# GLU over 8192 x 8192: the group's store and the reload of its buffer each issued as two transfers over even and odd partitions, and fewer, larger instructions per load

## The chip, the cores and the metric

The kernel runs on one core of a Trainium2 chip. The metric is the device time of one execution in microseconds. Before the change three timed runs gave 950.84 us as their median (947.65 to 954.41).

## The reference

The input `x` has 8192 rows of 8192 fp32 values. Each row is cut in two halves a and b, and the output, 8192 x 4096, is a times the sigmoid of b:

```python
def reference(x):
    a, b = np.split(x, 2, axis=-1)
    return a * (1 / (1 + np.exp(-b)))
```

The kernel reads 268.44 MB and writes 134.22 MB. There is one sigmoid and one multiplication per output value and no reuse of anything.

## The kernel before, in words

**Groups and halves.** The 8192 rows are cut into 16 groups of 512 rows. Of a group, each of the 128 partitions owns four neighbouring rows of x (128 KiB of device memory), split into two halves h = 0 and h = 1 of two rows each. A half is one load: 128 partitions by 64 KiB, 8.39 MB. The group's output, four packed rows of 16 KiB per partition, is again 64 KiB per partition, and normally leaves as one store of 8.39 MB.

**Three slots.** SBUF holds three buffers (slots) of 64 KiB per partition. Half 1 of every group uses slot 1. Half 0 uses slot 0 in even groups and slot 2 in odd groups, and the products of both halves are written packed into the slot of half 0, over data that has already been read. So slot 0 or 2 is loaded, worked on, filled with the whole group's output, stored, and only then loaded again, with half 0 of the group after the next one.

**Work.** `work` (L56) handles a quarter of a half at a time: 2048 columns of one of the two rows. ScalarE takes the sigmoid of b in place (L67), VectorE multiplies a by it and writes the product to its packed place (L71). Where a product would go over a value that an earlier product still has to read, the sigmoid waits for that product.

**Queues and waits.** All loads are issued from SyncE (L54), all stores from ScalarE (L78); each goes into the DMA queue of its issuing engine, and both queues are served by the same 16 DMA engines. The order of everything is the program's order, and most waits that the framework would add are taken out (`place`, L35); those that are left are these:

```python
load(g + 1, 1, [mul_of[g, 1, 3]])            # slot 1 is free after the group's last product
store(g, 2 if first else 0, 8, mul_of[g, 1, 3])
if g + 2 < n_groups:
    load(g + 2, 0, store_of[g])               # slot 0 or 2 is free when the store has landed
```

The first load is issued in two parts, and group 0 and the last group, 15, store in smaller pieces, so that the output starts and ends in small steps. The functions at the end of the program (`_launch_early`, `_close_on_sync`) move the first load ahead of the start barrier and shorten the end; the change doesn't touch them.

Of the kernel before, what the change touches and what calls it, by code (L numbers as in the profile page):

```python
# [6 lines left out]


def _tiles(ctx, tc, x, out):


    nc = tc.nc
    P = nc.NUM_PARTITIONS
    DEP = mybir.DependencyInfo(mybir.DependencyClass.Sync, mybir.DependencyReason.DATA)
    fp32 = mybir.dt.float32
    SIG = mybir.ActivationFunctionType.Sigmoid

    n_rows, n_cols = x.shape
    half = n_cols // 2
    quarter = half // 2  # L20
    R, H = 2, 2
    n_groups = n_rows // (P * R * H)
    x_t = x.rearrange("(g p h r) m -> g h p (r m)", p=P, h=H, r=R)
    out_t = out.rearrange("(g p q) m -> g p (q m)", p=P, q=H * R)

    pool = ctx.enter_context(tc.tile_pool(name="io", bufs=1))
    slots = [pool.tile([P, R * n_cols], fp32, name=f"x_sb{k}") for k in range(3)]
    traced = [[] for _ in slots]
    load_of, mul_of, store_of = {}, {}, {}

    def slot(g, h):
        return 1 if h else 2 * (g % 2)

    def place(touched, ins, *needs):


        kept = {n.ins.name for n in needs}
        seen = set()
        for k in touched:
            for e in traced[k]:  # L40
                if e.ins.name not in kept | seen:
                    seen.add(e.ins.name)
                    tc.declare_no_dep(ins.ins, e.ins, reason="follows from the waits that are kept")
            traced[k].append(ins)
        tc.keep_in_program_order(ins)
        return ins

    def load(g, h, needs=(), parts=1):

        width = R * n_cols // parts  # L50
        k = slot(g, h)
        for j in range(parts):
            c = slice(j * width, (j + 1) * width)
            ins = place([k], nc.sync.dma_start(out=slots[k][:, c], in_=x_t[g, h][:, c]), *needs)  # L54
            for r in range(R) if parts == 1 else [j]:
                load_of[g, h, r] = ins  # L56

    def work(g, h, k):

        r, c = k // 2, k % 2 * quarter  # L60
        of, to = slot(g, h), slot(g, 0)
        a = slots[of][:, r * n_cols + c : r * n_cols + c + quarter]
        b = slots[of][:, r * n_cols + half + c : r * n_cols + half + c + quarter]
        at = (h * R + r) * half + c
        before = {(0, 2): (g, 0, 0), (0, 3): (g, 0, 1), (1, 0): (g, 0, 3)}
        over = [mul_of[m] for m in [before.get((h, k))] if m]
        sig = nc.scalar.activation(out=b, in_=b, func=SIG)  # L67
        place([of], sig, load_of[g, h, r], *over)
        for m in over:
            tc.add_manual_dep(sig.ins, m.ins.name, DEP, reason="read before the product goes over it")  # L70
        mul = nc.vector.tensor_mul(out=slots[to][:, at : at + quarter], in0=a, in1=b)  # L71
        mul_of[g, h, k] = place(sorted({of, to}), mul, sig)

    def store(g, lo, hi, done):

        c = slice(lo * quarter, hi * quarter)
        k = slot(g, 0)
        ins = place([k], nc.scalar.dma_start(out=out_t[g][:, c], in_=slots[k][:, c]), done)  # L78
        store_of.setdefault(g, []).append(ins)

    load(0, 0, parts=2)
    load(0, 1)
    load(1, 0)
    for g in range(n_groups):
        first, final = g == 0, g == n_groups - 1
        for k in range(4):
            work(g, 0, k)
            if first and k == 1:
                store(g, 0, 2, mul_of[g, 0, 1])
        if final:  # L90
            store(g, 0, 2, mul_of[g, 0, 1])
            store(g, 2, 4, mul_of[g, 0, 3])
        for k in range(4):
            work(g, 1, k)
            if final and k > 0:
                store(g, 3 + k, 4 + k, mul_of[g, 1, k - 1])
        if final:
            store(g, 7, 8, mul_of[g, 1, 3])
            break
        load(g + 1, 1, [mul_of[g, 1, 3]])  # L100
        store(g, 2 if first else 0, 8, mul_of[g, 1, 3])
        if g + 2 < n_groups:
            load(g + 2, 0, store_of[g])


def _launch_early(nc):
# [68 lines left out]
@with_exitstack  # L175
def kernel(
    ctx: ExitStack,
    tc: tile.TileContext,
    x: bass.AP,
    out: bass.AP,  # L180
):
    nc = tc.nc
    with ExitStack() as pools:
        _tiles(pools, tc, x, out)
    tc.close()
    tc.compile()
    _launch_early(nc)
    _close_on_sync(nc)
# [30 lines left out]
```

## Time and profile before

| What | Value |
|---|---|
| Median of three timed runs | 950.84 us (947.65 to 954.41) |
| Profiled execution: its own time | 945.78 us |
| Profiled execution: its span | 944.4 us |
| Bytes moved, mean rate over the span | 402.67 MB, 426 GB/s |
| VectorE busy | 284.9 us, 128 multiplications of 128 x 2048 |
| ScalarE busy | 238.8 us, 128 sigmoids of 128 x 2048 and a table load |
| Loads (SyncE's queue) | 33 transfers: 2 of 4 MiB, 31 of 8 MiB |
| Stores (ScalarE's queue) | 22 transfers: 14 of 8 MiB, 1 of 6 MiB, 3 of 2 MiB, 4 of 1 MiB |
| Instructions | 374 |

The span is the profiled execution from its first to its last instruction; the execution's own time is 1.4 us longer, and the execution happens to be 5.1 us below the median of the timed runs. The span's 40 slices give a mean busy share of the 16 DMA engines; the queue table gives, for each DMA queue, its packets, its megabytes and the time that its packets took as a share of what 16 engines have in the span. The chain is the work that ended last, followed back from the end, in which "DMA" means time spent waiting for a transfer from its issue to its landing.

### The profile page before, as it was taken

How to read it: one execution, taken by the hardware profiler on the slowest of the kernel's cores; microseconds unless marked ns; L12 is line 12 of the kernel's file. 1: busy time of each engine (PE TensorE's matmuls, PEld its weight loads, DVE VectorE, ACT ScalarE, POOL GpSimd, SP SyncE). 2: the span in 40 equal slices, each digit the busy share in tenths (PEclk: the TensorE clock that was granted, in tenths of full speed). 3: DMA queues.
4: the chain of work that ended last, by engine and by line, in shares of the span. 5: the costliest groups of instructions: out<-in, count | busy, mean ns of one | idle time of the engine just before them, and what ended most of it. 6: DMA issues, size and time to landing. Idle time of an engine off the chain costs nothing.

```text
span 944.4 us, 374 instructions
## 1 busy us (share of the span) xinstructions
DVE 284.9 (30%) x128; ACT 238.8 (25%) x129; POOL 0.2 (0%) x4
## 2 busy tenths in 40 slices
DVE  1133332313323133331332313323133221332313
ACT  2132332203333033330333203333033320333203
POOL 0000000000000000000000000000000000000000
DMA  9999999999999999999999999999999999999998
GB/s 400 444 414 439 436 444 444 422 422 444 444 439 408 441 436 444 419 416 419 397 439 439 441 408 427 427 430 436 425 416 419 425 408 433 408 433 441 425 436 366
DMA packets 7922, 402.67 MB, mean 426 GB/s; under 512 B 880, under 2 KB 880, under 8 KB 880
## 3 DMA queue, kind: packets, MB, share of 16 engines
q1 hardware_dynamic: 4752, 268.44, 66.8%
q10 hardware_dynamic: 3168, 134.22, 32.8%
q14 instruction: 2, 0.02, 0.0%
HBM read 268.44 MB, written 134.22 MB: 426 GB/s over the span
## 4 chain that ended last, share of the span: by engine, by line
DMA 81%; DVE 15%; ACT 3%; issue 0%; ACTq 0%; SPq 0%
DMA x_sb<-in_x_dram 81%; DVE x_sb L71 15%; ACT x_sb L67 3%; ACTq L78 0%; SPq L54 0%; ACTq L67 0%
## 5 line engine op out<-in xcount | busy, mean ns | idle before, releaser
L71 DVE TENSOR_TENSOR x_sb<-x_sb 128x2048 f32<-128x2048 f32 x128 | 284.9, 2287 | 652.3 <-ACT x_sb L67 652.3
L67 ACT ACTIVATE x_sb<-x_sb 128x2048 f32<-128x2048 f32 x128 | 237.5, 1901 | 695.3 <-DMA x_sb<-in_x_dram 681.3
L67 ACT ACT_TABLE_LOAD x1 | 1.3, 1283 | 0.8 <-PEq L203 0.8
L203 POOL MEMSET const-bfloat16-1.0<- 128x1 bf16 x1 | 0.1, 101 | 0.0
L203 POOL MEMSET const-uint8-127<- 128x1 uint8 x1 | 0.1, 101 | 0.0
L203 POOL MEMSET const-float32-0.0<- 128x1 f32 x1 | 0.1, 98 | 0.2 <-issue 0.2
L203 POOL MEMSET const-float32-1.0<- 128x1 f32 x1 | 0.1, 98 | 0.0
## 6 DMA issues: line engine op xcount, KB each, us to landing
x_sb<-in_x_dram SPq DMA_DIRECT2D x2, 4096.0 KB, 16.4
out_dram<-x_sb ACTq DMA_DIRECT2D x3, 2048.0 KB, 33.3
out_dram<-x_sb ACTq DMA_DIRECT2D x1, 6144.0 KB, 38.0
out_dram<-x_sb ACTq DMA_DIRECT2D x4, 1024.0 KB, 6.9
x_sb<-in_x_dram SPq DMA_DIRECT2D x31, 45.0
out_dram<-x_sb ACTq DMA_DIRECT2D x14, 43.4
```

Source lines behind the costliest of these rows:

```text
L67: sig = nc.scalar.activation(out=b, in_=b, func=SIG)
L71: mul = nc.vector.tensor_mul(out=slots[to][:, at : at + quarter], in0=a, in1=b)
L203: nc = _bacc.Bacc("TRN2", target_bir_lowering=False, num_devices=1)
```

## The change

Three things are changed.

1. The group's store (groups 0 to 14) is issued as two transfers, one over the even partitions 0, 2, ..., 126 and one over the odd ones, 64 rows of 64 KiB each (48 KiB in group 0).
2. The reload of that slot, half 0 of the group after the next one, is issued as two transfers in the same way. The even one waits for the even store, the odd one for the odd store. Half 1 stays one transfer.
3. `work` covers a range of columns instead of a quarter. In groups 1 to 15 half 0 is one sigmoid and one multiplication over both rows (128 x 8192 elements); in groups 1 to 14 half 1 is two of each, one per row (128 x 4096). Group 0 keeps its quarters, and half 1 of group 15 too. With this the two stores of 2 MiB that follow half 0 of group 15 become one of 4 MiB.

```diff
+    everyone = slice(0, P)
+    by_two = [slice(0, P, 2), slice(1, P, 2)]
...
-    def load(g, h, needs=(), parts=1):
...
+    def load(g, h, p, c, *needs):
         k = slot(g, h)
...
+        ins = place([k], nc.sync.dma_start(out=slots[k][p, c], in_=x_t[g, h][p, c]), *needs)
+        for r in range(R):
+            if c.start < (r + 1) * n_cols and r * n_cols < c.stop:
+                load_of.setdefault((g, h, r), []).append(ins)
...
+    def work(g, h, lo, hi):
...
+        rows = slots[of].rearrange("p (r s m) -> p r s m", r=R, s=2)
+        packed = slots[to].rearrange("p (h r m) -> p h r m", h=H, r=R)[:, h]
+        if hi - lo == 8:
+            r, c = slice(0, R), slice(0, half)
+        else:
+            r = slice(lo // 4, lo // 4 + 1)
+            c = slice(lo % 4 * half // 4, (lo % 4 + hi - lo) * half // 4)
+        b = rows[:, r, 1, c]
...
         sig = nc.scalar.activation(out=b, in_=b, func=SIG)
...
+        mul = nc.vector.tensor_mul(out=packed[:, r, c], in0=rows[:, r, 0, c], in1=b)
...
+    def store(g, lo, hi, done, parts=(everyone,)):
...
+        for p in parts:
+            ins = place([k], nc.scalar.dma_start(out=out_t[g][p, c], in_=slots[k][p, c]), done)
+            store_of.setdefault(g, []).append(ins)
...
+        for lo, hi in fourths if first else [(0, 8)]:
+            work(g, 0, lo, hi)
...
         if final:
-            store(g, 0, 2, mul_of[g, 0, 1])
-            store(g, 2, 4, mul_of[g, 0, 3])
...
+            store(g, 0, 4, mul_of[g, 0, 8])
+        for k, (lo, hi) in enumerate(fourths if first or final else [(0, 4), (4, 8)]):
+            work(g, 1, lo, hi)
...
-        load(g + 1, 1, [mul_of[g, 1, 3]])
-        store(g, 2 if first else 0, 8, mul_of[g, 1, 3])
+        load(g + 1, 1, everyone, both, done)
+        store(g, 2 if first else 0, 8, done, by_two)
         if g + 2 < n_groups:
-            load(g + 2, 0, store_of[g])
+            for p, freed in zip(by_two, store_of[g][-2:]):
+                load(g + 2, 0, p, both, freed, *store_of[g][:-2])
```

## The prediction

> **What bounds the kernel now.** I read the page's slices and queue table first, because a kernel with no reuse can only be bound by its transfers or by a gap in them.
>
> ```profile
> span 944.4 us, 374 instructions
> DVE 284.9 (30%) x128; ACT 238.8 (25%) x129; POOL 0.2 (0%) x4
> ...
> DMA  9999999999999999999999999999999999999998
> ...
> q1 hardware_dynamic: 4752, 268.44, 66.8%
> q10 hardware_dynamic: 3168, 134.22, 32.8%
> ```
>
> No engine is busy for a third of the span, and the DMA engines are busy in all forty slices. The two queues' packets take 66.8 + 32.8 = 99.6% of what 16 engines have. So the time in which a DMA engine has nothing to do is 0.4% of 944.4 us, 3.8 us, and part of that is the start and the end. A transfer that is issued earlier can win no more than this.
>
> The same two lines give the price of a packet. Loads: 0.668 x 944.4 x 16 / (268.44 MB / 64 KiB = 4096) = 2.464 us per 64 KiB and engine. Stores: 0.328 x 944.4 x 16 / 2048 = 2.420 us. In the trace's own packet records a store of 64 KiB takes 2.42 us almost without exception, while some loads take 2.5 to 4.1. If every load went at the stores' pace, 4096 x 0.044 / 16 = 11.3 us would go. That is the second thing that could be won, and the floor is 6144 x 2.420 / 16 = 929.3 us of pure packets.
>
> Next the chain, by line and then in order of time, and SyncE's waits:
>
> ```profile
> DMA 81%; DVE 15%; ACT 3%; issue 0%; ACTq 0%; SPq 0%
> ```
>
> ```profile
> 100.07 1.92 ACT x_sb L67
> 101.99 0.02 issue
> 102.01 8.91 DVE x_sb L71 x4
> 110.92 0.02 issue
> 110.94 47.17 DMA x_sb<-in_x_dram
> 158.10 0.02 issue
> ```
>
> ```profile
> SPq L54 <- DMA out_dram<-x_sb: 595.3, 14, 44.3
> SPq L54 <- DVE x_sb L71: 268.5, 15, 55.0
> ```
>
> The reader is to see one period of 58 us (100.07 to 158.1): half 1 lands, is worked on for 10.9 us, its last product releases the load of the next half 1 and the store, and 47 us later that load lands. The chain passes through 10.9 us of compute per group (the 18%), but it is not what the chip waits for: while the compute runs, the queue still holds a load of half 0. In groups 0 to 13 SyncE waits for the store to land, up to 44.3 us each, then issues that load. It does so at 95.2, and the load of half 1 ahead of it in the same queue lands at 100.0; the last time it is 861.1 and 865.6. So the reload enters its queue 4.5 to 5 us before the queue runs dry. That is the reserve which the change enlarges.
>
> **The change part by part.**
>
> *Early reload.* The even store is half of the bytes and is first in ScalarE's queue, so it lands about halfway through the present 43 us, and the even reload is issued some 20 us earlier than now. But it stands behind half 1 in SyncE's queue, whose 16 engines are busy anyway. What it can take away is idle time of engines that run ahead: the trace's completion marks of one transfer lie 0.3 to 0.8 us apart until 300 us and up to 7 us afterwards, more than the reserve. All of that idle time is inside the 3.8 us, of which about 2 are start and end. Gain: 0 to 2 us; I take 0, since the engine that is last had no idle time.
>
> *More transfers.* Loads 33 to 47, stores 22 to 36 (28 groups' halves more, 15 for 15 groups, less one in the last group): 28 more, each with one small completion packet per engine. In the trace such a packet takes 9 ns: 28 x 0.009 = 0.25 us. Issuing costs 0.36 us more per group on ScalarE (its issues take 0.34 to 0.38) and 0.33 on SyncE, beside the 15 to 28 us that ScalarE waits for a load: nothing. The transfers use eight completion counters in turn, so each also waits for the one eight before it; with five per group instead of three that is one from a group and a half earlier, long landed. Behind the even reload's wait on SyncE stand the odd reload and then the next half 1; the odd store lands before that half 1 is due, as the whole store does today. No new stall.
>
> *Larger work, half 1.* Now the sequence after a landing is 1.92 + 8.91 = 10.9 us. With 4096 columns the first sigmoid ends later: at least the 1.92 of today, at most twice it, 3.84; the two multiplications are the same elements, at most 8.91. I take the upper end, 12.8 us, 1.9 more in each of groups 1 to 14. What hides it is the queued half 0: eight packets per engine at 2.42 are 19.4 us of work for the DMA engines when half 1 lands. Today 8.5 us of that are left at the next issue, then 6.6. Cost 0. If the cover were gone, 14 x 1.9 = 26.6 us.
>
> *Larger work, half 0.* One sigmoid (at most 4 x 1.90 = 7.6) and one multiplication (at most 9.1) after the landing, 16.7 instead of 11.1 us. Half 0 lands at 124.2, half 1 at 158.1, so there are 34 us for it. In group 15 the store of this half is issued at 890 + 17 = 907 instead of 896.4 and 901.1; the previous store occupies ScalarE's queue until 920. Cost 0. ScalarE and VectorE run 55 instructions each instead of 128.
>
> *The shape of the transfers.* This is the unknown. The trace shows only transfers over 128 partitions: 4752 packets over 33 loads are 144, that is 128 rows and 16 completions, so each of 16 engines carries eight rows. Afterwards 14 reloads (117.4 MB) and 15 stores (123.7 MB), 241.2 of 402.7 MB or 60%, go over 64 partitions at every second row. If such rows spread over the engines as evenly as the 128 do and no two engines get in each other's way, a row takes its 2.42 us: cost 0. At worst half of the engines, or of the paths into SBUF, serve them at a time, since half of the partitions are named: the 241.2 MB at half of 433.3 GB/s (16 x 64 KiB in 2.42 us) cost 557 us more. Below zero, the reads may lose part of their 11.3 us. I take 0, the nearest row being that of a 64 KiB row of 2.42 us, which the change keeps.
>
> Of the Trainium skill, "SBUF — State Buffer", section "Door 1: The DMA port swizzle", bears on this: a transfer's rate depends on how many of 16 SBUF ports its partitions reach, and neighbouring fours share a port, so even partitions reach all 16, while 0 to 63 reach eight, measured there at 196 GB/s against 328; by that the sum is unchanged. Against the change speaks its summary rule, "Use 128 partitions; one DMA, not several", and that "DMA: Bandwidth & Descriptors", "The descriptor swizzle", gives each engine one port of its own only for a 128-partition transfer. If the 64 rows were dealt out in neighbouring fours, an engine's rows would cross two ports and two engines would meet at each; by that the 557 us would apply as far as they run in step. No run here shows a 64-partition transfer.
>
> *Sum.* Profiled execution: 945.8 + 0.25 + 0 = 946. The median of the timed runs is 5.1 us above it, time that I put to the loads' variable packets and leave as it is: **951 us**.
>
> **The rivals.**
>
> *A, forecast: hidden anyway.* The DMA engines move the same packets at the same pace. For it: 99.6% busy, equal row length. Against it: nothing in the trace shows the new shape. 951, chance 0.50, own range 942 to 960.
>
> *B, the loads lose their long packets.* Half of the loads walk memory with twice the step between rows, and engines that never run dry may stay in step, as in the first 300 us, where loads too take 2.42. Price: at most -11.3, to 939.5; to be faster by over 1% (9.5 us, about what a measurement of this kernel can tell from no change), 84% of it must go. Against: loads that the change leaves alone, half 1, have the long packets too. Chance 0.14.
>
> *C, the other side: two engines meet on one path.* In the 64-row transfers, one part of the engines waits for another at SBUF. Every 1% on their 2.42 us costs 5.57 us; from 1.7% (2.46 us) on the kernel is slower by over 1%. Full collision gives 951 + 557 = 1508, collision a quarter of the time 1090. For it: 60% of the bytes and no slack, so that any loss is paid in full. Against it: of every eight neighbouring partitions, four are in each half, so no region of SBUF is left out. Chance 0.30: 0.12 up to 990 (7%), 0.18 above.
>
> *D, the cover of the compute is gone.* Engines that are up to 7 us ahead empty the queue before the 12.8 us are over; where all do, 951 + 26.6 = 977. It decides once the reserve of 6.6 us is used up in most groups. Against it: the slowest engine sets the time and has its queue full. Chance 0.06.
>
> That the change fails to separate the halves I exclude: the even reload waits only for the even store (in group 0 also for its first small store), and the odd one for the odd.
>
> **How the numbers follow.** The forecast is A. The range takes in B down to 938, A, D and C up to 990, and leaves out 0.02 below and 0.18 above, with the 557 us among what is left out. Faster by over 1%: B, 0.14. Within: A, 0.50. Slower: C and D, 0.36.
>
> **What would show it.** Packets 7922 + 28 x 16 = 8370. ScalarE's queue at 2.42 us per 64 KiB again (share x span x 16 / 2048): A; above 2.46: C, and SyncE's queue, half of it in the new shape, rises with it. Loads below 2.43: B. Slices of DMA below 9 around the landings: D. Compute from a landing of half 1 to the next load 12 to 13 us; SyncE's waits for stores 28 instead of 14. The prediction is wrong if the new shape has a pace of its own.

## The result and the profile after

The changed kernel takes 981.59 us in the median (970.17 to 982.48) against 949.5 us for the kernel before (four runs, 947.65 to 954.41): ratio of the means 1.030, 95% interval 1.022 to 1.039. It is slower by 3%. The forecast was 951 us, no difference; the time lies inside the range of 938 to 990. A ratio leaves out runs that took over 1.5% longer than the fastest of the same kernel, which happened in two experiments below, twice the delay and halves. The profiled execution is the fastest of the four, 970.17 us; the other three took 11 to 12 us longer, and what they lost beyond it no profile shows.

The page of the changed kernel: span, busy time of the engines, the DMA engines' slices, the two queues (packets, megabytes, share of 16 engines) and the chain by engine.

```profile
span 968.7 us, 299 instructions
DVE 279.9 (29%) x55; ACT 228.7 (24%) x56; POOL 0.2 (0%) x4
...
DMA  9999999999999999999999999999999999999998
...
q1 hardware_dynamic: 4976, 268.44, 66.9%
q10 hardware_dynamic: 3264, 134.22, 32.4%
...
DMA 79%; DVE 14%; ACT 6%; issue 0%; ACTq 0%; SPq 0%
```

The slices look the same as before, all nines. The shares have to be turned into durations to see anything: loads 0.669 x 968.7 x 16 / 4096 = 2.531 us per 64 KiB (2.464 before), stores 0.324 x 968.7 x 16 / 2048 = 2.452 us (2.420 before), and 0.7% of the span, 6.8 us, without a packet (3.8 before). A packet here is one row of a transfer, up to 64 KiB, on one of the 16 engines. Longer load packets are 0.067 x 4096 / 16 = 17.2 us, longer store packets 4.1 us, idle time 3.0 us: together the 24.3 us by which the span grew. The extra time sits in the transfers, and mostly in the loads.

SyncE's waits and one period of the chain (start, length, what) after:

```profile
SPq L54 <- DMA out_dram<-x_sb: 658.1, 28, 29.8
SPq L54 <- DVE x_sb L81: 220.5, 15, 55.0
```

```profile
163.03 3.62 ACT x_sb L77
166.65 0.02 issue
166.68 8.77 DVE x_sb L81 x2
175.46 49.06 DMA x_sb<-in_x_dram
224.53 0.02 issue
```

28 waits for stores instead of 14, as the change intends, and 12.4 us from the first sigmoid on half 1 to the next issue instead of 10.9. The new rows by form confirm both lengths:

```profile
L81 DVE TENSOR_TENSOR x_sb<-x_sb 128x4096 f32<-128x4096 f32 x28 | 122.7, 4422 | 331.2 <-ACT x_sb L77 331.2
L77 ACT ACTIVATE x_sb<-x_sb 128x4096 f32<-128x4096 f32 x28 | 99.7, 3608 | 402.3 <-DMA x_sb<-in_x_dram 402.3
```

**Where in the period the time is lost.** The trace's packet records were sorted by their distance from the issue of the group's store, which is also the issue of the next half 1. "Long" is the time over 2.418 us per 64 KiB (the median packet of both kernels), in loads and stores, "idle" the time without a packet, both as a mean of the 16 DMA engines and summed over the same twelve periods in each kernel, from the store of group 1 to that of group 13. The first and the last column hold the two handovers, the moments at which a queue that has little left gets a new transfer.

| kernel | first 16 us (store and half 1 begin): long / idle | 16 to 44 us | from 44 us on (reload of half 0 begins) |
|---|---|---|---|
| before | 5.2 / 0.0 | 0.2 / 0.0 | 4.0 / 1.3 |
| changed | 20.6 / 2.4 | 5.3 / 0.3 | 0.1 / 0.0 |

So the early reload did what it was made for, the 5.3 us at the reload's handover are gone. The loss arose at the other handover, and in the middle of the period. Loads that run while no engine stores take 2.421 us in the changed kernel (before 2.458); the others take 2.605 (before 2.469). Which loads lengthen can be read by dealing the packets out to the 16 engines in the order of their queues (about one packet in seventy does not fit): half 1, a transfer over 128 partitions as before, takes 2.62 us per packet in the mean (2.43 before), the even and odd reloads 2.42 and 2.45 (the whole reload 2.50 before). So the loads that grew are not those that were cut.

### The profile page after: what moved, and what is told of

It is laid out like the page before. It is cut to its first block, busy times and chain, and to the rows that moved or that the text cites. A ratio compares the mean times of both kernels' runs of the same rounds, so it can differ in the third digit from the quotient of the medians.

```text
span 968.7 us, 299 instructions
## 1 busy us (share of the span) xinstructions
DVE 279.9 (29%) x55; ACT 228.7 (24%) x56; POOL 0.2 (0%) x4
## 2 busy tenths in 40 slices
DMA packets 8242, 402.67 MB, mean 416 GB/s; under 512 B 1328, under 2 KB 1328, under 8 KB 1328
## 4 chain that ended last, share of the span: by engine, by line
DMA 79%; DVE 14%; ACT 6%; issue 0%; ACTq 0%; SPq 0%
DMA x_sb<-in_x_dram 79%; DVE x_sb L81 14%; ACT x_sb L77 6%; ACTq L89 0%; SPq L54 0%; ACTq L77 0%
## 5 line engine op out<-in xcount | busy, mean ns | idle before, releaser
L81 DVE TENSOR_TENSOR x_sb<-x_sb 128x4096 f32<-128x4096 f32 (+2 forms) x55 | 279.9, 5121 | 680.8 <-ACT x_sb L77 680.8
L77 ACT ACTIVATE x_sb<-x_sb 128x4096 f32<-128x4096 f32 (+2 forms) x55 | 227.4, 4169 | 728.9 <-DMA x_sb<-in_x_dram 727.7
```

The costliest lines, as they stand in the source:

```text
L81: mul = nc.vector.tensor_mul(out=packed[:, r, c], in0=rows[:, r, 0, c], in1=b)
```

## The experiments

Four theories stood against each other at first. **S**: the store over every second partition lengthens the loads beside it. **R**: the reload in that shape costs. **W**: the larger work costs, since all that it releases is issued later. **P**: more and earlier transfers cost, whatever their shape. All edits are shown against the changed kernel. Where "quarters" is written, this edit is in, which gives back the work of the kernel before:

```diff
-        for lo, hi in fourths if first else [(0, 8)]:
+        for lo, hi in fourths:
...
-            store(g, 0, 4, mul_of[g, 0, 8])
+            store(g, 0, 2, mul_of[g, 0, 4])
+            store(g, 2, 4, mul_of[g, 0, 8])
-        for k, (lo, hi) in enumerate(fourths if first or final else [(0, 4), (4, 8)]):
+        for k, (lo, hi) in enumerate(fourths):
```

All ratios are to the kernel before, run in the same session, with 95% intervals.

### The larger work alone

```diff
-        store(g, 2 if first else 0, 8, done, by_two)
+        store(g, 2 if first else 0, 8, done)
...
-            for p, freed in zip(by_two, store_of[g][-2:]):
-                load(g + 2, 0, p, both, freed, *store_of[g][:-2])
+            load(g + 2, 0, everyone, both, *store_of[g])
```

> The larger sigmoids and multiplications alone, with whole stores and whole reloads as before the change. The changed kernel's page has 24 us more span than before, 21 of them in longer packets, almost all of them loads that run while other engines store. Theory S (the stores over every second partition lengthen the loads beside them) expects no difference from the kernel before: ratio 0.995 to 1.005, loads at 2.46 us per 64 KiB. Theory W (the later issue after half 1, 12.4 us instead of 10.9, starves or unsettles the queue) expects most of the loss here: ratio 1.015 to 1.03. Theory R (the reload over every second partition is what costs) and theory P (more, earlier transfers bring the engines out of step) expect no difference.

Measured: 966.62 us, ratio 1.020 (1.015 to 1.025). W is right that this part costs by itself, which the prediction had at nothing. Long load packets and idle time, from the page of this run:

```profile
span 962.1 us, 228 instructions
...
q1 hardware_dynamic: 4752, 268.44, 66.9%
q10 hardware_dynamic: 3024, 134.22, 32.3%
```

Loads 0.669 x 962.1 x 16 / 4096 = 2.514 us, stores 2.428 us as before, 0.8% or 7.7 us idle. By the sorting of the table above: 12.8 us long in the first 16 us, and 5.9 long and 6.9 idle from 44 us on. Both handovers are worse than before. Nearly all of the idle time lies at the second handover, the reload of half 0; when the next half 1 and the store are issued, packets are long but no engine is without one (0.0 idle).

### The store alone in two parts

Whole reload as in the run above, split store, quarters.

> The store alone in even and odd partitions; the reload is whole and waits for both, and the work is in quarters as before the change. Theory S expects all of the loss: ratio 1.02 to 1.035, loads of half 1 at 2.55 us or more per 64 KiB. Theories R and W expect 0.995 to 1.005. Theory P, by which the earlier issue matters, expects at most a third of the loss, 1.00 to 1.01, since nothing is issued earlier.

Measured: 998.42 us, ratio 1.055 (1.051 to 1.059), more than the whole change. S holds, and the size is larger than the 1.02 to 1.035 that it expected.

```profile
span 996.2 us, 417 instructions
...
DMA  9999999989999999999999999999999899998998
...
q1 hardware_dynamic: 4752, 268.44, 66.5%
q10 hardware_dynamic: 3408, 134.22, 31.7%
```

1.8% of the span, 17.9 us, are idle here, and the slices show it: eights among the nines. Loads take 2.588 us. All loads are of the old shape in this run (4752 packets on q1, as before): what is longer are loads that were not cut at all. In the period: 15.6 us long in the first 16, 17.1 from 16 to 44, and from 44 on 7.0 long and 13.8 idle. Against the kernel before that is 10.4 us more in the first part, 18.2 in the second and 15.5 in the third, idle time included. Here the reload waits for the later of two stores and is issued 2.5 us ahead of the landing of half 1 instead of 4.9 (medians). The delay runs below lose time in this third part without a split store, so the 15.5 us may come from the late reload and not from the shape; this run alone doesn't part the two.

### The reload alone in two parts

```diff
-        store(g, 2 if first else 0, 8, done, by_two)
+        store(g, 2 if first else 0, 8, done)
...
-            for p, freed in zip(by_two, store_of[g][-2:]):
-                load(g + 2, 0, p, both, freed, *store_of[g][:-2])
+            for p in by_two:
+                load(g + 2, 0, p, both, *store_of[g])
```

Quarters, and both parts wait for the whole store.

> The reload alone in even and odd partitions, both waiting for the whole store; work in quarters. Theory R expects the loss: ratio 1.02 to 1.035. Theory S and theory W expect no loss, 0.99 to 1.005; since loads that ran while nobody stored took 2.421 us in the changed kernel against 2.458 before, S allows a gain of up to 4 us. Theory P expects at most 1.01.

Measured: 951.99 us, ratio 1.0045 (1.002 to 1.008). R is out as the main cause: reloading every second partition costs half a per cent, a sixth of what is to be explained.

### The same early handover, cut by columns

```diff
-        store(g, 2 if first else 0, 8, done, by_two)
+        store(g, 2 if first else 0, 4, done)
+        store(g, 4, 8, done)
...
-            for p, freed in zip(by_two, store_of[g][-2:]):
-                load(g + 2, 0, p, both, freed, *store_of[g][:-2])
+            for c, freed in zip([row0, row1], store_of[g][-2:]):
+                load(g + 2, 0, everyone, c, freed, *(store_of[g][:-2] if c is row0 else []))
```

Quarters. The two parts are the first and the second 32 KiB of all 128 partitions.

> Store and reload in two transfers each as in the change, with the same early reload, but cut by columns: 128 partitions of 32 KiB instead of 64 partitions of 64 KiB; work in quarters. Theories S and R, by which the choice of partitions costs, expect no loss: ratio 0.99 to 1.005. Theory P (two transfers and an earlier reload cost, whatever their shape) expects most of the loss, 1.015 to 1.035. Theory W expects 0.995 to 1.005.

Measured: 935.08 us (934.99 to 935.53), ratio 0.987 (0.984 to 0.991): faster than the kernel before, and steadier. P is out: the number of transfers and the early reload don't cost. But the edit did one thing more than was meant. The first half of the store holds no product of half 1, so no wait for the last product was made, and it was issued when half 1 had landed, 10.8 us before the second half. The next run separates this.

### Cut by columns, the first half of the store held back

```diff
             ins = place([k], nc.scalar.dma_start(out=out_t[g][p, c], in_=slots[k][p, c]), done)
+            tc.add_manual_dep(ins.ins, done.ins.name, DEP, reason="no earlier than this product")
```

On top of the cut by columns.

> The cut by columns again, but with its first half of the store held back until the group's last product, as in the change. In the run before, that half left 10.8 us earlier, when half 1 had landed, because it doesn't contain the last products. Theory Q (32 KiB rows over all 128 partitions, and a reload that is issued while half of the store still runs, are what avoids the long packets) expects 0.985 to 0.99 again, a span of 933 to 936. Theory E (what helped is the earlier start of the store, so that store and next load aren't issued at the same moment into a nearly empty queue) expects the gain to go: 0.997 to 1.01, with long loads again 2 to 4 us after the store's issue.

Measured: 943.45 us (937.61 to 945.27), ratio 0.994 (0.992 to 0.997). It lies between: the cut by columns is still a little faster than the kernel before without the earlier store, and the earlier store brings the rest.

```profile
span 935.9 us, 443 instructions
...
q1 hardware_dynamic: 6768, 268.44, 66.6%
q10 hardware_dynamic: 5328, 134.22, 33.3%
```

What stays of theory Q is the packets: loads take 0.666 x 935.9 x 16 / 4096 = 2.435 us, and there are next to no long packets at either handover, although the reload of the second half is issued some 10 us after half 1 has landed in every other group and close to the landing in the others (median 5.4 us after). This profile is of the fastest of the ten runs, 937.61 us, and doesn't show what the others lose. A late second reload thus doesn't explain the long packets by itself; the cut of the store and the reload has its part. How large that part is, the run called even and odd parts with quarters of work shows below: its stores, reloads and waits come in the same order, only the cut differs, and it takes 1.043 and 1.047 where this one takes 0.994. (The cuts differ in two ways, 128 partitions and rows of 32 KiB, and which of them counts was not tried; rows of 64 KiB alone are not it, since the whole stores of the kernel before have them.)

### The issue later by 1.5 us, nothing else

```diff
+    spare = pool.tile([P, 1400], fp32, name="spare")
+    nc.vector.memset(spare[:], 0.0)
...
         done = mul_of[g, 1, 8]
+        if not final:
+            done = nc.vector.tensor_mul(out=spare[:], in0=spare[:], in1=spare[:])
```

Whole stores and reloads, quarters; the next load of half 1 and the store wait for the spare product.

> The kernel before, with a spare multiplication of about 1.55 us on VectorE between a group's last product and the issue of the next load of half 1 and of the store (128 x 1400 elements in a buffer of their own; results are unchanged). Theory T (the larger work costs its 2% because the issue comes 1.55 us later, so that the reload in the queue is nearly used up and the engines wait at the two handovers) expects the time of the run with the larger work alone: ratio 1.015 to 1.025, with idle DMA time and long first packets of the reloads. Theory L (it is the larger instructions themselves, which take SBUF or the queue away from the transfers) expects 0.997 to 1.005.

Measured: 966.23 us, ratio 1.018 (1.014 to 1.022), the same as the larger work alone (1.020). One period of its chain:

```profile
219.31 1.92 ACT x_sb L81
221.23 0.02 issue
221.25 8.90 DVE x_sb L85 x4
230.15 1.54 DVE spare L118
231.69 0.02 issue
231.70 49.59 DMA x_sb<-in_x_dram
```

So it is the time of issue, T, and not the size of the instructions, L. The delay, 1.52 us in each of 15 groups or 22.8 us, costs 17. In the period: 14.8 us long in the first 16, and from 44 on 5.8 long and 5.7 idle, the picture of the larger work. The reload is issued 2.9 us ahead of the landing of half 1 where it was 4.9 before, and in the worst group 0.1 us behind it.

### Twice the delay

The same with 128 x 2890 elements.

> The kernel before with a spare multiplication twice as long (128 x 2890, about 3.1 us) ahead of the issue of the next load of half 1 and of the store. With 1.55 us it was 1.018. Theory T (the reload is issued some 4.5 us before the queue runs dry and about 2 to 3 us of that are needed; all later issue beyond the rest is paid in full, in each of 14 groups) expects another 14 x 1.55 = 21.7 us: 1.035 to 1.045, with idle DMA time above 20 us at the reload's handover. If the cost were a fixed one of any disturbance, it stays at 1.015 to 1.025.

Measured: 988.31, 989.39, 1004.08 and 1012.59 us; the ratio of the two shorter runs is 1.043 (1.038 to 1.048). The second delay of about 1.56 us in 15 groups, 23.4 us, costs by these two 2.5% or 23.5 us: about its full price. The profiled execution, 1004.08 us, shows where: some slices fall to sixes and sevens, and over the twelve periods the engines are idle for 31.0 us from 44 us on, where the single delay had 5.7.

```profile
DMA  9999999999979999799997999979999699999998
```

T stands; a fixed price is out.

### Even and odd parts with quarters of work

> Parts 1 and 2 of the change, the even and odd stores and reloads with the early reload, but the work in quarters as before. The store alone in two parts was 1.055, the changed kernel 1.030. If the early reload gives back what the store alone lost at the handover (18.9 us of idle DMA time there, 6.5 in the changed kernel), this is below 1.030: 1.01 to 1.025, with idle time under 6 us. If the larger work had been a help inside the change, it is above: 1.03 to 1.05.

The only edit is the one called quarters.

Measured: 988.64 us, ratio 1.043 (1.037 to 1.048). Inside the change the larger work is no loss but, if anything, a gain: 1.030 (1.022 to 1.039) with it. That is the opposite of its effect on whole stores (1.020). The two effects of this edit aren't additive, and why the later issue suits the split store was not settled.

### The same once more

The two reloads were to wait for both stores:

```diff
-            for p, freed in zip(by_two, store_of[g][-2:]):
-                load(g + 2, 0, p, both, freed, *store_of[g][:-2])
+            for p in by_two:
+                load(g + 2, 0, p, both, *store_of[g])
```

> Even and odd stores and even and odd reloads with the work in quarters, but both reloads wait for both stores, so that nothing is issued earlier than with one store. The same with the early reload was 1.043, the split store with a whole reload 1.055. If the early reload is worth what these two differ by, this is 1.05 to 1.06 with over 15 us of idle DMA time, most of it 44 to 52 us after the store's issue; if the reload's shape made that difference, it is 1.04 to 1.047.

Measured: 992.59 us, ratio 1.047 (1.042 to 1.051). This edit failed as an experiment: the even reload touches nothing that the odd store reads, so no wait was made, and the instructions and waits are those of the run before. It is a repetition of it, and shows how far two runs of one program lie apart: 1.043 and 1.047. What the early reload is worth within this shape is therefore known only from the store alone in two parts (1.055, whole late reload) against these two: about 1%, with what the reload's own cut costs already taken off.

### Halves instead of even and odd

```diff
-    by_two = [slice(0, P, 2), slice(1, P, 2)]
+    by_two = [slice(0, P // 2), slice(P // 2, P)]
```

Quarters.

> As the run before this one, but the two parts are the partitions 0 to 63 and 64 to 127 instead of the even and the odd ones. If any transfer over 64 partitions costs the same (its issue and its descriptors), the ratio is that of the even and odd parts within 0.01. If what matters is which partitions a transfer reaches, this is much slower: 64 neighbouring partitions reaching half of the paths would give up to 1.5; and if every second row is what disturbs, it is faster, 0.99 to 1.005.

Measured: 1411.77 us (median of 1396.05 to 1438.75), ratio 1.482 (1.468 to 1.496).

```profile
span 1407.2 us, 441 instructions
...
DMA  9999999999989989799999799996999999999797
...
q1 hardware_dynamic: 4976, 268.44, 70.3%
q10 hardware_dynamic: 3408, 134.22, 25.6%
```

Loads take 0.703 x 1407.2 x 16 / 4096 = 3.86 us per 64 KiB, and those that run while nobody stores 5.07 in the median, twice 2.42, as if two engines took turns. In the changed kernel loads that run while nobody stores take 2.421, so even and odd partitions have nothing of this kind, at least when they run alone.

### The store's parts to neighbouring rows

```diff
-            ins = place([k], nc.scalar.dma_start(out=out_t[g][p, c], in_=slots[k][p, c]), done)
+            to = {0: slice(0, P // 2), 1: slice(P // 2, P)}[p.start] if p.step else p
+            ins = place([k], nc.scalar.dma_start(out=out_t[g][to, c], in_=slots[k][p, c]), done)
```

On top of the store alone in two parts; the output's rows come out in another order.

> The store from even and odd partitions as in the run of the split store alone (1.055), whole reload, work in quarters, but each part is written to 64 neighbouring rows of the output instead of every second one, so the output's rows come out in another order. If the long packets come from the step of 128 KiB between the rows written, this is 1.00 to 1.02; if they come from the partitions read or from the transfers' number and issue, it stays at 1.045 to 1.065.

Measured: 1002.13 us, ratio 1.058 (1.054 to 1.062). It stays at the price of the split store (1.055). The step between the rows written isn't the cause; what is left is the partitions read, or that 64 of them make one transfer.

### The change with its cut by columns

The cut by columns as above, with the larger work of the change.

> The change with its cut by columns in place of even and odd partitions: early reload, store and reload in two transfers of 128 x 32 KiB each, and the larger work. With quarters of work the cut by columns was 0.987. Theory T expects the larger work to cost little here, since a reload that is issued while half of the store still runs has a large reserve: 0.985 to 0.995. If the 1.55 us are paid whatever the reserve, it is 1.00 to 1.01.

Measured: 935.11 us (934.87 to 935.34), ratio 0.986 (0.983 to 0.990). This kernel is faster than both, by 1.4% than the one before and by 4.7% than the changed one (935.11 / 981.59, two sessions).

```profile
span 933.1 us, 283 instructions
...
DMA  9999999999999999999999999999999999999999
...
q1 hardware_dynamic: 6768, 268.44, 66.7%
q10 hardware_dynamic: 5184, 134.22, 33.3%
```

The queues fill the whole span, with loads at 2.431 us and stores at 2.427. All that the first bound left, 929.3 us of packets and a few us at the ends, is reached. The later issue, worth 2% with whole stores, costs nothing here: the two reloads are issued 35.1 and 12.1 us ahead of the landing of half 1 (medians). In the period 1.7 us are long in all, and 0.02 idle (before 9.4 and 1.3).

## Why the prediction was right or wrong

**What bounds it: right.** The DMA engines do, and 929.3 us of packets are the floor: the best kernel has a span of 933.1. That the loads' long packets were 11.3 us to be won was right too; the cut by columns won them, not the change.

**Early reload, "gain 0 to 2 us; I take 0": the mechanism right, too small.** At its handover it took away 5.3 us in the middle groups, not only the idle 1.3, since 4.0 us more were long packets. But "the odd store lands before that half 1 is due" failed: the odd reload is issued 0.6 us after half 1 has landed (median), where the whole reload had been 4.9 ahead. And the step had looked at one handover alone; what was gained there reappeared at the other.

**More transfers, 0.25 us: harmless, as the cut by columns shows, but the issue was mis-sized.** A store over every second partition takes 0.48 and 0.62 us to issue, not 0.36, a reload 0.47, not 0.33. The packets came to 8242, not 8370: the last group's two stores that became one also save 128 data packets.

**Larger work, half 1, "cost 0": this step failed for that part by itself.** The sizes were near: 12.4 us instead of the 12.8 taken. What failed is the cover that was reckoned with. I set 1.9 us against the 8.5 us of half 0 that are queued at the next issue. The same later issue also comes off the 4.5 to 5 us by which the reload is issued before the queue runs dry, a number that stood in the prediction for another purpose (it was read in two groups; over all of them it is 3.2 to 6.1). The reading is that fewer rows of half 0 are left ahead of half 1, so half 1 ends earlier against the store. Measured is that this reserve fell to 3.5 us with the larger work and to 2.9 with the delay (medians), and to nothing in single groups. The measured price, 2.0%, some 19 us, and 1.8% for the bare delay, is close to what the prediction gave if "the cover were gone", 14 x 1.9 = 26.6. In the change itself it isn't paid on top; there the sum of the parts fails.

**The shape of the transfers, "cost 0": this is the term that made the forecast wrong.** The store in two parts alone, with its later reload, costs 5.5%, store and reload 4.3 to 4.7%; with the cut by columns in their place the same kernel takes 0.994, and 0.986 with the larger work and the earlier store. I took the nearest row, a 64 KiB row of 2.42 us, and that row nearly stayed: stores take 2.452, reloads running alone 2.421. What the row can't tell is what a transfer does to another. Most of the price is paid by the loads beside it, 17.2 us of the 24.3; the store's own packets have 4.1.

**The range held by luck.** The forecast in it was "no difference", and the kernel is slower by 3%. What carries the range up to 990 are the rivals C and D, and the loss measured, in the 128-partition loads of half 1 beside a store, is in neither.

**The rivals.** B (939.5, shorter loads) did not come with the change. C priced the 64-row transfers' own packets, and they are not what lengthened most in the changed kernel: its size is in C's lower band (up to 990), but ScalarE's queue, C's sign, is at 2.452 us, below the 2.46 that was set (2.467 with the store alone in two parts), and the even and odd reloads take 2.42 and 2.45 us, while half 1, which C left out, takes 2.62. Whether half 1 waits at SBUF for the store's rows was not shown either way. The doubled packets of the halves, 5.07 us, are the size that C describes, and its worst case of 1508 us was near for them (1412). "SBUF — State Buffer", "Door 1", of the Trainium skill agrees with both: by its rule even partitions reach all ports and 0 to 63 only half. The prediction's reading of "DMA: Bandwidth & Descriptors", "The descriptor swizzle", by which even rows might meet at a port, is not supported: those reloads take 2.421 us alone. The rule "one DMA, not several", from the section "Summary: rules for kernel authors" of the first page, did not hold here: with store and reload in two transfers of 32 KiB rows each the kernel was 1.4% faster than with one, and 0.6% with the store's first half held back. D, the lost cover, has the right size for the larger work alone, 19 us of its 26.6, but not the place: no engine ran empty at the issue (0.0 us idle), the packets there were long, and the idle 6.9 us lie at the reload's handover.

**What stays open.** In the kernels whose group stores have rows of 48 or 64 KiB, load packets that begin within a few us of the store's issue are long on all or most of the 16 engines at once (3.3 to 3.7 us in one group of the larger work alone): in some groups before, in nearly every group with a split store or a later issue, and hardly ever with rows of 32 KiB (0.6 to 0.8 us in the first 16 us of the twelve periods together). What the load packets wait for there, and why partitions at every second place make it worse, was not shown; nor were even and odd partitions tried with rows of 32 KiB, which would part the two differences between the cuts. In the store alone in two parts a second such stall, of 1.1 us in the loads, comes about 30 us after the store's issue, with no issue near it.

## What to carry to other kernels

Where transfers fill the time, look at the handovers, not at the busy share: turn each queue's share into a time per packet, and set any later issue against the smallest reserve on its way, not against the largest. When a transfer is cut in two so that its buffer comes free earlier, try the cut along the rows, across all partitions, first: here it was the one that gained. A row that keeps its own duration is no evidence that it leaves its neighbours alone.

## What was unexpected of the hardware

- A store from every second partition in 64 KiB rows takes 2.47 us per row, but the 128-partition loads of the same run lengthen from 2.46 to 2.59 us in the mean, with stalls of 1.1 to 1.5 us in some 16 packets at once; writing its rows side by side changes nothing (1.055 and 1.058).
- A delay of 1.5 us per group in the issue, beside DMA engines that were 99.6% busy, cost 17 us in all, and the next 1.5 us another 23.
- With stores and reloads in rows of 32 KiB, and the store's first half leaving early, the timed runs lie within 0.5 us of each other (934.87 to 935.34, 934.99 to 935.53); before the change they lay 7 us apart, after it 12.
- With transfers over 64 neighbouring partitions a 64 KiB packet takes 5.07 us in the loads that run beside no store, half the rate.
